# Attention scores of a first mixer: three products over 64 rows per head, two heads in turn on the array's row halves, in place of two products of stacked parts

## The chip, the core and the metric

The kernel runs on one core of a Trainium2 chip. Five engines work side by side, each through its own instruction queue in order: TensorE (PE, matrix products; its weight loads are shown apart as PEld), VectorE (DVE), ScalarE (ACT), GpSimd (POOL) and SyncE (SP, which here only starts transfers). The metric is the device time of one execution in microseconds (us). The kernel before takes 1453.77 us, the median of three runs that lie between 1453.04 and 1455.49 us. The profile was taken from one further execution.

## The reference, cut to what matters

The program is a two-layer streaming encoder on 512 tokens of width 1024, batch 1. Layer 0 starts with a mixer of two kinds of attention. Both have a query and key width of 64:

```
def forgetting_attention(q, k, v, log_f):          # 8 heads
    ...
        logits = jnp.einsum('bhqd,bhkd->bhqk', q_b, k, preferred_element_type=jnp.float32) * scale
        logits = logits + F_b[..., :, None] - F[..., None, :]
        logits = jnp.where(k_pos[None, :] <= q_pos[:, None], logits, NEG_INF)
        p = jax.nn.softmax(logits, axis=-1)
        return jnp.einsum('bhqk,bhkd->bhqd', p.astype(v.dtype), v)

def differential_attention(q1, q2, k1, k2, v, lam): # 4 heads, two score maps each
    ...
        l1 = jnp.einsum('bhqd,bhkd->bhqk', q1_b, k1, preferred_element_type=jnp.float32) * scale
        l2 = jnp.einsum('bhqd,bhkd->bhqk', q2_b, k2, preferred_element_type=jnp.float32) * scale
        p1 = jax.nn.softmax(jnp.where(mask, l1, NEG_INF), axis=-1)
        p2 = jax.nn.softmax(jnp.where(mask, l2, NEG_INF), axis=-1)
        p = p1 - lam * p2
        return jnp.einsum('bhqk,bhkd->bhqd', p.astype(v.dtype), v)
```

The change touches only how `q·k` of these two is formed. The rest of layer 0 (output projection, cross-attention to a memory of 256 tokens, a gated feed-forward net) and layer 1 are as they were.

## The kernel before

**Precision.** A float32 operand `v` is split in two parts of the fast matrix format, `hi` (a rounded copy, made by ACT) and `lo = v - hi` (a subtraction on DVE, line 279). A product of two split operands is three products, hi·hi, hi·lo and lo·hi (`mm3`, lines 289 to 291). Nearly all matrix work of the program has this form.

**Scores.** A projection of q or k yields a 128 x 512 tile: 128 rows are the 64 channels of two heads (or of the two maps of a differential head) one above the other, and the 512 columns are tokens. There are 8 such pairs of tiles, 4 for the differential heads and 4 for the forgetting heads; the text calls each a q/k pair. `q_parts` (line 616) and `k_parts` (629) scale a projection's result into the tile `tmp` (lines 619 and 632) and then build operands for each head s that fill all 128 rows with parts: `qa` holds q-hi on the head's own 64 rows and q-lo on the other 64; `ka` holds k-hi twice; `kb` holds k-lo on the head's own rows and zeros on the others, which four MEMSETs at line 751 write once at the start. `p_soft` (657) then makes the scores of 128 queries against n = 128, 256, 384 or 512 keys (i = 0 to 3) with two full products: ka·qa gives hi·hi + hi·lo in one, kb·qa adds lo·hi (lines 669 and 670). A product has at least 256 columns. So one q/k pair takes, for each i, two heads times two products of 256, 256, 384 and 512 columns, and the stage has 8 x 4 = 32 such places.

**What follows a score.** One DVE instruction at line 676 adds the mask or bias, takes the row minimum and clears the bank of the result; ACT takes the exponential (682), DVE its reciprocal (683). Forgetting heads are normalised on DVE (909), differential pairs combined (841, 842), the result is turned by PE in 128 x 128 blocks (700, `ident`), copied (703, 705), and multiplied with v: full products at line 712 for the differential heads, and for the forgetting heads at line 922 products with 64 columns of weights, two heads in turn on the array's two column halves.

**Order.** All of this stage is put in order by a planner (`Plan`). Each piece of work has a priority, a guessed PE duration and guessed ACT and DVE times, and takes resources: two banks `s` for scores (shared with small helper products at 417, 452, 612), two banks `w`, eight score tiles `e`. Work without hurry, the next projections (`acc<-xh`, lines 289 to 291) and the products of the memory (`acc<-mem`), stands between the scores. On top of the planner's order the framework that builds the program moves an instruction back when what it waits for comes late. In the trace the stage lies between 0 and about 235 us; its scores lie between 48 and 219 us.

Of the kernel before, what the change touches and what calls it, by code (L numbers as in the profile page):

```python
# [237 lines left out]
class Builder:  # L238
# [377 lines left out]
    def q_parts(self, ps):  # L616
        nc, mp = self.nc, self.mp
        tq = self.til(mp, "tmp")
        nc.vector.scalar_tensor_tensor(out=folded(tq[:]), in0=restored(ps[:]), scalar=-0.125, in1=folded(self.rb[:]), op0=ALU.mult, op1=ALU.mult)
        out = []  # L620
        for s in range(2):
            a, b = slice(64 * s, 64 * s + 64), slice(64 - 64 * s, 128 - 64 * s)
            qa = self.til(mp, f"qa{s}", dtype=F32R, bufs=2)
            nc.scalar.copy(qa[a, :], tq[a, :])
            self.sub(qa[b, :], tq[a, :], qa[a, :])
            out.append(qa)
        return out

    def k_parts(self, ps, par):
        nc, mp = self.nc, self.mp  # L630
        tk = self.til(mp, "tmp")
        nc.vector.tensor_tensor(out=folded(tk[:]), in0=restored(ps[:]), in1=folded(self.rb[:]), op=ALU.mult)
        out = []
        for s in range(2):
            a, b = slice(64 * s, 64 * s + 64), slice(64 - 64 * s, 128 - 64 * s)
            ka = self.til(mp, f"ka{s}", dtype=F32R, bufs=2)
            kb = self.kbt[s][par]
            nc.scalar.copy(ka[a, :], tk[a, :])
            nc.scalar.copy(ka[b, :], tk[a, :])
            self.sub(kb[a, :], tk[a, :], ka[a, :])  # L640
            out.append((ka, kb))
        return out

    def p_qk(self, pl, dq, dk, par, kdeps, edeps, prio):
# [3 lines left out]
            pl, dq, self.xs, lambda ps: st.update(q=self.q_parts(ps)), (("D", 0.66), ("A", 0.52), ("D", 0.6), ("D", 0.6)), load=(("A", 0.52),),  # L648
# [3 lines left out]
            pl, dk, self.xs, lambda ps: st.update(k=self.k_parts(ps, par)), (("D", 0.6), ("A", 0.52), ("D", 0.6), ("D", 0.6)), load=(("A", 1.56),),  # L652
# [4 lines left out]
    def p_soft(self, pl, st, s, i, bias, deps, prio):  # L657

        nc, mp = self.nc, self.mp
        n = P * (i + 1)  # L660
        nn = max(n, 256)
        res = {}

        def score():
            qa, (ka, kb) = st["q"][s], st["k"][s]
            ps = self.bank("s")
            b = bias()
            qs = qa[:, i * P : (i + 1) * P]
            nc.tensor.matmul(banked(ps[:, :nn]), qs, alternate(ka[:, :nn]), start=True, stop=False)
            nc.tensor.matmul(banked(ps[:, :nn]), qs, alternate(kb[:, :nn]), start=False, stop=True)  # L670
            e = res["e"] = self.x[self.turns % 8]
            self.turns += 1
            got = restored(ps[:, :nn])
            to, got, b = (e[:, :n], got[:, 0, :], b) if n < nn else (folded(e[:, :n]), got, folded(b))
            sm = res["sm"] = self.til(self.sp, "sm", (P, 4), bufs=12)
            nc.vector.tensor_tensor_reduce(
                out=to, in0=got, in1=b, scale=1.0, scalar=3.0e38, op0=ALU.add, op1=ALU.min, accum_out=sm[:, 0:1]
            )

        def expo():  # L680
# [4 lines left out]
        a = pl.add(score, 2 * MM * nn / 512, deps, prio, take=("s", "e"), free=("s",), chain=(("D", 0.07 + 0.54 * n / 512),))  # L685
        b = pl.add(expo, 0, [a], prio, chain=(("A", 0.3 + 0.4 * n / 512), ("D", 0.08)))
# [57 lines left out]
    def mix0(self):  # L744
        nc, t, tc = self.nc, self.t, self.tc
        with tc.tile_pool(name="mix0", bufs=1, reuse_waits="tile") as mp:
            self.mp = mp
            self.kbt = [[mp.tile([P, 512], F32R, name=f"kb{s}{i}") for i in range(2)] for s in range(2)]
            for s in range(2):
                for i in range(2):  # L750
                    nc.vector.memset(self.kbt[s][i][64 - 64 * s : 128 - 64 * s, :].bitcast(F32), 0.0)
# [72 lines left out]
            for h in range(4):  # L824
# [3 lines left out]
                st, qk = self.p_qk(pl, t["dq"][h], t["dk"][h], h % 2, xk, [norm], p)  # L828
# [3 lines left out]
                for i in range(4):  # L832
                    n = P * (i + 1)
                    bias = lambda n=n: dmask[:, 512 - n : 512]
                    r1, a1, b1 = self.p_soft(pl, st, 0, i, bias, qk, p + SOFT_PRIO)
                    r2, a2, b2 = self.p_soft(pl, st, 1, i, bias, qk, p + SOFT_PRIO)
# [8 lines left out]
                    ss += [a1, a2]  # L845
# [26 lines left out]
            for p_ in range(4):  # L872
# [4 lines left out]
                st, qk = self.p_qk(pl, t["fq"][p_], t["fk"][p_], p_ % 2, xk, [norm], p)  # L877
# [16 lines left out]
                for i in range(4):  # L894
                    n = P * (i + 1)
                    for h, s, pt, fb, b, got, ts in items:

                        def bias(i=i, n=n, fb=fb):
                            fm = self.til(mp, "tb")
                            nc.gpsimd.affine_select(  # L900
                                out=fm[:, :n], in_=fb["b"][:, :n], pattern=[[-1, n]], compare_op=ALU.is_ge, fill=BIG, base=i * P, channel_multiplier=1
                            )
                            return fm[:, :n]

                        r1, a1, b1 = self.p_soft(pl, st, s, i, bias, qk + [b], p + SOFT_PRIO)

                        def norm1(r1=r1, n=n):
                            e, sm = r1["e"], r1["sm"]
# [925 lines left out]
```

## Time and profile before

| what | value |
|---|---|
| median of three runs | 1453.77 us (1453.04 to 1455.49) |
| the profiled execution | 1455.27 us |
| its span, from the first to the last instruction | 1453.5 us |
| PE busy | 1427.1 us, 98% |
| DVE busy | 1193.3 us, 82% |
| ACT busy | 801.7 us, 55% |
| mean granted PE clock | 0.998 |

The profiled execution is 1.5 us slower than the median, and 1.8 us of its time lie outside the span. A change in the trace is therefore added to 1455.27 us for the profiled execution and to 1453.77 us for the median.

How to read the rows: `L669` is line 669 of the kernel; `s<-ka,qa` is a product of the moving tile ka and the weights qa into a bank s; `128*128 128x256` are the rows and columns of the weights and the size of the moving tile. Matrix products overlap in the array, so a product's duration (0.38 us for 512 columns) is longer than the time that it takes from the engine. That is read from one start to the next, and the text calls it a slot.

### The profile page before, as it was taken

The numbers are of one execution on the slowest core, as the hardware profiler recorded it, in microseconds if no ns is written. First come the engines' busy times: TensorE is split into PE (matmuls) and PEld (weight loads), VectorE is DVE, ScalarE is ACT, GpSimd is POOL, SyncE is SP. The second block draws the span as 40 slices with busy tenths as digits, with TensorE's granted clock in tenths as the row PEclk, the third lists the DMA queues.
The fourth block names the chain that finished last, engine by engine and source line by source line (L and its number), as shares of the span: only waits on it lengthen the run. The fifth ranks groups of instructions, "written<-read, shape, count | busy, mean of one in ns | idle before, by whom it ended". The sixth has DMA issues, their size and how long they took to land.

```text
span 1453.5 us, 22202 instructions
## 1 busy us (share of the span) xinstructions
PE 1427.1 (98%) x8330; PEld 1267.4 (87%) x8330; DVE 1193.3 (82%) x2255; ACT 801.7 (55%) x1345; POOL 57.9 (4%) x100
## 2 busy tenths in 40 slices
PE   9999999999999999999999999999999999999998
PEld 7888868899889999899888788889988899999987
DVE  7778886766689999999778868676667999999975
ACT  7767574444466555545456734444445655555544
POOL 0000120000001000000000100000000000000000
PEclk9999999999999999999999999999999999999999
DMA  5222304324248666542332232323323756564322
GB/s 200 88 73 73 102 32 158 117 86 131 87 138 196 172 156 166 145 131 66 94 103 87 74 102 78 111 91 127 117 87 123 200 156 168 159 160 133 89 70 80
DMA packets 60796, 171.74 MB, mean 118 GB/s; under 512 B 6673, under 2 KB 6673, under 8 KB 60689
## 3 DMA queue, kind: packets, MB, share of 16 engines
q1 hardware_dynamic: 55072, 152.43, 32.3%
q0 software_dynamic: 4608, 16.78, 6.9%
q8 instruction: 65, 1.06, 0.3%
q10 hardware_dynamic: 1008, 1.12, 0.2%
q14 instruction: 43, 0.34, 0.1%
HBM read 168.21 MB, written 2.10 MB: 117 GB/s over the span
## 4 chain that ended last, share of the span: by engine, by line
PE 68%; DVE 22%; issue 4%; ACT 4%; DMA 1%; POOL 0%; DVEq 0%; ACTq 0%; POOLq 0%
PE acc L289 13%; PE acc L291 13%; PE acc L290 13%; DVE wl L279 5%; DVE c L1281 4%; PE w L289 3%; PE w L290 3%; PE w L291 3%; PE acc L351 2%; PE s L289 2%; PE acc L352 2%; PE acc L353 2%; PE s L291 2%; PE s L290 2%; PE w L1621 1%
## 5 line engine op out<-in xcount | busy, mean ns | idle before, releaser
L289 PE MATMUL acc<-xh,wh 128*128 128x512 f32 (+1 forms) x832 | 293.3, 353 | 0.1
L291 PE MATMUL acc<-xh,wl 128*128 128x512 f32 (+1 forms) x832 | 289.1, 347 | 1.3 <-DVE wl L279 1.3
L290 PE MATMUL acc<-xl,wh 128*128 128x512 f32 (+1 forms) x832 | 289.0, 347 | 0.0
L279 DVE TENSOR_TENSOR wl<-raw,wh 128x1024 fp32r<-128x1024 f32 (+2 forms) x201 | 240.6, 1197 | 39.3 <-ACT wh L282 35.8
L282 ACT CAST wh<-raw 128x1024 fp32r<-128x1024 f32 (+2 forms) x137 | 140.3, 1026 | 156.2 <-PE acc L290 96.7
L291 PEld LDWEIGHTS acc<-xh,wl 128*128 128x128 f32 x832 | 158.2, 190 | 16.8 <-DVE wl L279 1.6
L289 PEld LDWEIGHTS acc<-xh,wh 128*128 128x128 f32 x832 | 158.2, 190 | 15.4 <-ACT v L1393 0.3
L290 PEld LDWEIGHTS acc<-xl,wh 128*128 128x128 f32 x832 | 158.2, 190 | 15.0
L1281 DVE SCALAR_TENSOR_TENSOR c<-hs,vec,c 128x512 f32<-128x512 f32 x176 | 129.3, 750 | 5.1 <-ACT c L1274 4.6
L289 PE MATMUL w<-ah,wh 128*128 128x512 f32 x304 | 115.6, 380 | 0.0
L291 PE MATMUL w<-ah,wl 128*128 128x512 f32 x304 | 115.3, 379 | 0.0
L290 PE MATMUL w<-al,wh 128*128 128x512 f32 x304 | 115.3, 379 | 0.0
L1274 ACT ACTIVATE c<-hs,vec 128x512 f32<-128x512 f32 x88 | 69.7, 812 | 56.5 <-DVE hs L1419 49.2
L291 PEld LDWEIGHTS w<-ah,wl 128*128 128x128 f32 x304 | 57.5, 189 | 8.1
L289 PEld LDWEIGHTS w<-ah,wh 128*128 128x128 f32 x304 | 57.7, 190 | 7.2 <-ACT c L1289 0.5
L290 PEld LDWEIGHTS w<-al,wh 128*128 128x128 f32 x304 | 57.7, 190 | 6.7
L289 PE MATMUL acc<-mem,wh 128*128 128x256 f32 (+1 forms) x192 | 60.3, 314 | 0.0
L291 PE MATMUL acc<-mem,wl 128*128 128x256 f32 (+1 forms) x192 | 59.8, 311 | 0.0
L290 PE MATMUL acc<-mem,wh 128*128 128x256 f32 (+1 forms) x192 | 59.6, 311 | 0.0
L512 DVE TENSOR_TENSOR x<-w,x 128x512 f32<-128x512 f32 x72 | 49.5, 688 | 9.1 <-PE w L291 9.1
L1183 ACT CAST wh<-dr 128x512 fp32r<-128x512 f32 x64 | 39.4, 615 | 31.1 <-PE w L290 15.3
L512 DVE TENSOR_TENSOR x<-acc,x 128x512 f32<-128x512 f32 x32 | 22.1, 691 | 40.4 <-PE acc L291 40.4
(373 smaller groups left out, 3758.5 us busy)
## 6 DMA issues: line engine op xcount, KB each, us to landing
raw<-in_up_dram SPq DMA_DIRECT2D x56, 512.0 KB, 3.3
dr<-in_down_dram SPq DMA_DIRECT2D x64, 256.0 KB, 2.9
sa<-in_up_dram SPq DMA_DIRECT2D x32, 512.0 KB, 4.2
sa<-in_up_dram POOLq DMA_DIRECT2D x32, 512.0 KB, 5.5
raw<-in_xk_dram SPq DMA_DIRECT2D x16, 512.0 KB, 3.3
raw<-in_wo_dram SPq DMA_DIRECT2D x16, 512.0 KB, 3.2
raw<-in_xq_dram SPq DMA_DIRECT2D x16, 512.0 KB, 3.3
raw<-in_xv_dram SPq DMA_DIRECT2D x16, 512.0 KB, 3.2
```

Of the source, the lines that this page charges most:

```text
L279: self.nc.vector.tensor_tensor(out=lo, in0=v, in1=hi.bitcast(F32), op=ALU.subtract)
L282: self.nc.scalar.copy(hi, v)
L289: mm(out, wh, xh, start=first, stop=False, skip_group_check=parts)
L290: mm(out, wh, xl, start=False, stop=False, skip_group_check=parts)
L291: mm(out, wl, xh, start=False, stop=last, skip_group_check=parts)
L351: mm(ps, xh[k][:, ts], wh, start=(k == 0), stop=False)
L352: mm(ps, xh[k][:, ts], wl, start=False, stop=False)
L353: mm(ps, xl[k][:, ts], wh, start=False, stop=(k == 7))
L512: self.nc.vector.tensor_tensor(out=x, in0=restored(ps[:]), in1=x, op=ALU.add)
L1183: nc.scalar.copy(st["wh"][:, :cols], st[tag][:, :cols])
L1274: nc.scalar.activation(st["c_"][:, j, :], hs()[:, j, 2:514], AF.Identity, scale=self.col("cw", (layer * 3 + 2) * 44 + blk), bias=self.col( ...
L1281: nc.vector.scalar_tensor_tensor(out=c, in0=hs()[:, j, n : n + 512], scalar=w, in1=c, op0=ALU.mult, op1=ALU.add)
```

## The change

The parts stay in the plain form: `qh`, `ql`, `kh`, `kl`, 128 x 512 each, one ACT copy and one DVE subtraction for q, and the same for k. A score is three products with the 64 rows of its own head: rows 0 to 63 for one, 64 to 127 for the other. The two heads of a q/k pair are now one piece of work in the planner: it takes both `s` banks and two `e` tiles at once, emits the six products in turn between the heads, each placed on the row half of the array (`tile_position=(64 * s, 0)`), and then the two DVE reductions. The planner counts 3 slots of PE for it where it counted 2 + 2.

```
-        out = []
-        for s in range(2):
-            a, b = slice(64 * s, 64 * s + 64), slice(64 - 64 * s, 128 - 64 * s)
-            qa = self.til(mp, f"qa{s}", dtype=F32R, bufs=2)
-            nc.scalar.copy(qa[a, :], tq[a, :])
-            self.sub(qa[b, :], tq[a, :], qa[a, :])
-            out.append(qa)
-        return out
-
-    def k_parts(self, ps, par):
...
-            nc.scalar.copy(ka[a, :], tk[a, :])
-            nc.scalar.copy(ka[b, :], tk[a, :])
-            self.sub(kb[a, :], tk[a, :], ka[a, :])
-            out.append((ka, kb))
-        return out
+        return self.qk_parts("q", tq)
+
+    def k_parts(self, ps):
+        tk = self.til(self.mp, "tmp")
+        self.nc.vector.tensor_tensor(out=folded(tk[:]), in0=restored(ps[:]), in1=folded(self.rb[:]), op=ALU.mult)
+        return self.qk_parts("k", tk)
+
+    def qk_parts(self, tag, v):
+        hi, lo = (self.til(self.mp, tag + i, dtype=F32R) for i in "hl")
+        self.split(hi[:], lo[:], v[:])
+        return hi, lo
...
-            nc.tensor.matmul(banked(ps[:, :nn]), qs, alternate(ka[:, :nn]), start=True, stop=False)
-            nc.tensor.matmul(banked(ps[:, :nn]), qs, alternate(kb[:, :nn]), start=False, stop=True)
...
+            ps = [self.bank("s") for _ in range(2)]
+            bs = [bias() for bias in biases]
+            for c, (q, k) in enumerate(((0, 0), (1, 0), (0, 1))):
+                for s in range(2):
+                    rows = slice(64 * s, 64 * s + 64)
+                    nc.tensor.matmul(
+                        banked(ps[s][:, :nn]), st["q"][q][rows, i * P : (i + 1) * P], alternate(st["k"][k][rows, :nn]), start=(c == 0), stop=(c == 2),
+                        tile_position=(64 * s, 0),
+                    )
+            for s in range(2):
...
-        a = pl.add(score, 2 * MM * nn / 512, deps, prio, take=("s", "e"), free=("s",), chain=(("D", 0.07 + 0.54 * n / 512),))
-        b = pl.add(expo, 0, [a], prio, chain=(("A", 0.3 + 0.4 * n / 512), ("D", 0.08)))
+        a = pl.add(score, 3 * MM * nn / 512, deps, prio, take=("s", "s", "e", "e"), free=("s", "s"), chain=(("D", 0.07 + 0.54 * n / 512),) * 2)
+        b = [pl.add(lambda r=r: expo(r), 0, [a], prio, chain=(("A", 0.3 + 0.4 * n / 512), ("D", 0.08))) for r in res]
...
-            self.kbt = [[mp.tile([P, 512], F32R, name=f"kb{s}{i}") for i in range(2)] for s in range(2)]
-            for s in range(2):
-                for i in range(2):
-                    nc.vector.memset(self.kbt[s][i][64 - 64 * s : 128 - 64 * s, :].bitcast(F32), 0.0)
```

Three places of the programs show what the new order is. The first is PE's queue at the first score of the first differential head (i = 0). Before, between two groups of projection products:

```order
L291 MATMUL acc_83_501<-xh_28_218,wl_496 128x512
L669 MATMUL s_521<-ka_78_487,qa_71_448 128x256
L670 MATMUL s_521<-kb_110,qa_71_448 128x256
L669 MATMUL s_526<-ka_79_491,qa_72_451 128x256
L670 MATMUL s_526<-kb_112,qa_72_451 128x256
L289 MATMUL acc_83_501<-xh_30_224,wh_496 128x512
```

And after, where 501 and 502 are the two heads' banks:

```order
L291 MATMUL acc_83_487<-xh_23_197,wl_483 128x512
L658 MATMUL s_501<-kh_477,qh_440 128x256
L658 MATMUL s_502<-kh_477,qh_440 128x256
L658 MATMUL s_501<-kh_477,ql_441 128x256
L658 MATMUL s_502<-kh_477,ql_441 128x256
L658 MATMUL s_501<-kl_478,qh_440 128x256
L658 MATMUL s_502<-kl_478,qh_440 128x256
L289 MATMUL acc_83_487<-xh_25_203,wh_482 128x512
```

Four full products have become six on row halves, and full products stand on both sides of them. Of the 32 places 24 keep the strict turn of the heads, three begin with two products of one head, and five have all three products of one head ahead of the other's. The second place is one of these five, in PE's queue at the second q/k pair of the forgetting heads. Before, a head's two products stood by themselves, with turns (`ident`) between the heads:

```order
L289 MATMUL acc_495_2274<-mem_1590,wh_2351 128x256
L669 MATMUL s_1956<-ka_304_1536,qa_288_1469 128x256
L670 MATMUL s_1956<-kb_113,qa_288_1469 128x256
L700 MATMUL w_1965<-ident,x_139 128x128 x4
L669 MATMUL s_1974<-ka_303_1532,qa_287_1466 128x256
L670 MATMUL s_1974<-kb_111,qa_287_1466 128x256
```

After, banks 1937 and 1938 of one place (i = 0):

```order
L290 MATMUL acc_529_2447<-mem_1650,wh_2442 128x256
L692 MATMUL w_1957<-ident,x_131 128x128 x2
L658 MATMUL s_1937<-kh_1520,qh_1506 128x256
L658 MATMUL s_1937<-kh_1520,ql_1507 128x256
L658 MATMUL s_1937<-kl_1521,qh_1506 128x256
L692 MATMUL w_1957<-ident,x_131 128x128
L658 MATMUL s_1938<-kh_1520,qh_1506 128x256
L658 MATMUL s_1938<-kh_1520,ql_1507 128x256
L658 MATMUL s_1938<-kl_1521,qh_1506 128x256
```

The heads are apart here, and one place makes two excursions to the row halves. In all the 32 places stand in 38 unbroken runs. Counting each boundary in PE's queue between full products, column halves (line 922) and row halves, there were 14 before, all at line 922, and there are 79 after.

The third place is DVE's queue at the first q/k pair. Before, with two subtractions of 64 x 512 each for q and for k:

```order
L619 SCALAR_TENSOR_TENSOR tmp_446<-acc_69_421,rb_325 128x512
L279 TENSOR_TENSOR wl_561<-raw_559,wh_560 128x1024
L279 TENSOR_TENSOR qa_71_448<-tmp_446,qa_71_448 64x512
L279 TENSOR_TENSOR qa_72_451<-tmp_446,qa_72_451 64x512
L632 TENSOR_TENSOR tmp_485<-acc_76_460,rb_325 128x512
L279 TENSOR_TENSOR wl_625<-raw_623,wh_624 128x1024
L279 TENSOR_TENSOR kb_110<-tmp_485,ka_78_487 64x512
L279 TENSOR_TENSOR kb_112<-tmp_485,ka_79_491 64x512
```

After:

```order
L619 SCALAR_TENSOR_TENSOR tmp_438<-acc_69_413,rb_317 128x512
L279 TENSOR_TENSOR wl_552<-raw_550,wh_551 128x1024
L279 TENSOR_TENSOR ql_441<-tmp_438,qh_440 128x512
L624 TENSOR_TENSOR tmp_475<-acc_76_450,rb_317 128x512
L279 TENSOR_TENSOR wl_631<-raw_629,wh_630 128x1024
L279 TENSOR_TENSOR kl_478<-tmp_475,kh_477 128x512
```

One subtraction of 128 x 512 stands where two of 64 x 512 stood. ACT's queue loses four copies per q/k pair: two of q become one, four of k become one. The queue of GpSimd keeps its order; in SyncE's queue the two loads of the memory and the loads of the first output weights shift by a few places against the loads of the projections.

73 lines of the change are left out of this document (31 added, 42 removed).

## The prediction

> **What bounds the kernel now.** I read the page's busy times first, then the stage of the scores in stretches of 10 us, then single products of PE in the timeline. The page:
>
> ```profile
> PE 1427.1 (98%) x8330; PEld 1267.4 (87%) x8330; DVE 1193.3 (82%) x2255; ACT 801.7 (55%) x1345; POOL 57.9 (4%) x100
> PE 68%; DVE 22%; issue 4%; ACT 4%; DMA 1%; POOL 0%; DVEq 0%; ACTq 0%; POOLq 0%
> ```
>
> PE bounds the program: 98% busy, and 68% of the chain that ended last. So each slot that PE gains or loses counts in full, except where PE waits anyway. In the stage of the scores it waits little. These are all its waits over 0.1 us there, from the view of waits between 80 and 230 us, and two of the 10 us stretches with the lowest granted clock (columns: stretch, length, busy time and number of instructions of PE, PEld, DVE, ACT, POOL, then PE's clock, DMA share, GB/s):
>
> ```profile
> PE w L700 <- DVE x L909: 1.6, 2, 1.4
> PE s L452 <- DVE sqt L446: 1.3, 4, 0.4
> PE s L669 <- DVE sm L676: 1.0, 2, 0.7
> PE w L700 <- DVE sm L683: 0.2, 1, 0.2
> ...
> 190.00:200.00 10.00, 8.16 (x51) 5.73 (x49) 9.22 (x31) 9.73 (x25) 2.79 (x6) 0.94 0.01 2
> 200.00:210.00 10.00, 10.00 (x61) 7.48 (x61) 7.76 (x25) 4.90 (x15) 1.72 (x4) 0.89 0.16 53
> ```
>
> The waits sum to 4.1 us in 150 us, all of them for DVE. A clock of 0.94 and 0.89 costs 0.06 x 10 + 0.11 x 10 = 1.7 us more. So at most 5.8 us of the stage are to be had from DVE and ACT; the rest is PE's own work.
>
> **The products themselves (term A).** Slots, from start to start in the timeline:
>
> ```profile
> 48.04 0.28 PE L670 MATMUL s<-kb,qa 128*128 128x256 f32 x1
> 48.15 0.28 PE L669 MATMUL s<-ka,qa 128*128 128x256 f32 x1
> ...
> 51.58 0.33 PE L670 MATMUL s<-kb,qa 128*128 128x384 f32 x1
> 51.74 0.33 PE L669 MATMUL s<-ka,qa 128*128 128x384 f32 x1
> ...
> 57.36 0.38 PE L669 MATMUL s<-ka,qa 128*128 128x512 f32 x1
> 57.57 0.38 PE L670 MATMUL s<-kb,qa 128*128 128x512 f32 x1
> ```
>
> A slot is 0.11, 0.16 and 0.21 us for 256, 384 and 512 columns. Per q/k pair the four places have widths of 256, 256, 384 and 512 columns, 0.59 us for one product of each; four products make 2.36 us, and 8 pairs 18.9 us. The change makes six of the four. If two halves run at the same time, six cost three slots: 14.2 us, a gain of 4.7. If they run one after the other, six slots: 28.3 us, a loss of 9.4. No product on row halves stands in this trace. The nearest rows are the products on column halves, line 922:
>
> ```profile
> 182.87 0.28 PE L670 MATMUL s<-kb,qa 128*128 128x256 f32 x1
> 183.08 1.07 PE L922 MATMUL w<-pt,v 128*64 128x512 f32 x2
> 184.08 0.43 PE L669 MATMUL s<-ka,qa 128*128 128x384 f32 x1
> 184.34 0.33 PE L670 MATMUL s<-kb,qa 128*128 128x384 f32 x1
> 184.60 2.37 PE L922 MATMUL w<-pt,v 128*64 128x512 f32 x14
> 186.90 0.33 PE L700 MATMUL w<-ident,x 128*128 128x128 f32 x1
> ...
> 94.78 0.38 PE L353 MATMUL acc<-wh,xl 128*128 128x512 f32 x1
> 94.99 2.32 PE L712 MATMUL w<-pt,v 128*128 128x512 f32 x8
> 97.15 0.27 PE L700 MATMUL w<-ident,x 128*128 128x128 f32 x1
> ```
>
> Plain float32 products are two records each. At line 712 four of them on the whole array, 512 + 384 + 256 + 128 = 1280 columns, take 97.15 - 94.99 = 2.16 us. At line 922 the x14 are one of 512 columns and two each of 384, 256 and 128, 2048 columns; one after the other they would take 2.16 x 2048 / 1280 = 3.46 us, but they take 186.90 - 184.60 = 2.30, which is the 2.16 of the busier half and a little. Column halves do run together, and I take the same for row halves. The Trainium skill, "TensorE: Matmul & The Clock Gate", Part 3, says that products on different row groups run at the same time, their starts about 4 ns apart; by that rule alone the sum would be the gain of 4.7 us, and no run here shows it for rows.
>
> The gain is not whole: in five of the 32 places (two of 512 columns, three of 256) the program has all three products of one head first. They need three slots more each: 2 x 3 x 0.21 + 3 x 3 x 0.11 = 2.3 us. Term A: -4.7 + 2.3 = **-2.4 us**.
>
> **The switches (term B).** The same rows show what it costs to change between the whole array and halves. The product at 182.87 has a slot of 0.11 and would let the next start at 182.98; line 922 starts at 183.08, 0.10 later. One product of 512 columns would take 2.16 x 512 / 1280 = 0.86 us; back on the whole array, 184.08 is 1.00 later, 0.14 more: 0.05 for its weights, which could not be loaded ahead, and about 0.10 for the change back. The product at 184.08 then holds PE for 0.26 us instead of 0.16: again 0.10 for weights, now of 128 columns. At 184.34 + 0.16 = 184.50 the next change begins, and line 922 starts at 184.60. So a change costs 0.10, and 0.10 more for 128 columns of weights that come in the open; the row halves have 128 columns as well. I price a switch at 0.20 us. From below it is bounded by the whole-array change to line 712 at 94.99, 0.21 after the product ahead and so without any gap: 0. The Trainium skill, "TensorEngine Tiling (Array Packing)", Key Properties, has a rule against this change: switching the tiling mode drains the engine. The trace agrees with its 0.10 us of gap; the page gives no price.
>
> The order has 79 boundaries where 14 stood: 65 x 0.20 = 13.0 us. Against it stands what the scores pay now: the first product of a score often shows its weight load in the open, because it waited for its bank:
>
> ```profile
> L669 PE MATMUL s<-ka,qa 128*128 128x256 f32 (+2 forms) x64 | 22.4, 356 | 1.1 <-DVE sm L676 1.0
> L670 PE MATMUL s<-kb,qa 128*128 128x256 f32 (+2 forms) x64 | 20.0, 317 | 0.0
> ```
>
> The first is 356 - 317 = 39 ns longer than the second, x 64 = 2.5 us, which the switches replace. Term B: 13.0 - 2.5 = **+10.5 us**.
>
> **DVE and ACT (term C).** Between 0 and 230 us:
>
> ```profile
> L279 DVE TENSOR_TENSOR qa<-tmp,qa 64x512 fp32r<-64x512 f32 x16 | 11.0, 687 | 0.7 <-ACT qa L624 0.2
> L279 DVE TENSOR_TENSOR kb<-tmp,ka 64x512 fp32r<-64x512 f32 x16 | 10.9, 684 | 0.5 <-ACT ka L638 0.2
> L279 DVE TENSOR_TENSOR qa<-w,qa 128x512 fp32r<-128x512 f32 x1 | 0.7, 693 | 2.7 <-ACT qa L282 2.7
> L639 ACT CAST ka<-tmp 64x512 fp32r<-64x512 f32 x16 | 9.9, 617 | 0.4
> L638 ACT CAST ka<-tmp 64x512 fp32r<-64x512 f32 x16 | 9.9, 616 | 0.8 <-DVE tmp L632 0.6
> L624 ACT CAST qa<-tmp 64x512 fp32r<-64x512 f32 x16 | 9.8, 614 | 2.8 <-PE s L670 1.5 <-DVE tmp L619 1.1
> ...
> 195.13 0.38 PE L290 MATMUL acc<-ml,wh 128*128 128x512 f32 x1
> 196.93 0.63 PE L700 MATMUL w<-ident,x 128*128 128x128 f32 x4 [1.42 <-DVE x L909]
> 197.89 0.38 PE L669 MATMUL s<-ka,qa 128*128 128x256 f32 x1 [0.33 <-DVE sm L676]
> ...
> 194.54 0.69 DVE L279 TENSOR_TENSOR qa<-tmp,qa 64x512 fp32r<-64x512 f32 x1
> 195.70 0.68 DVE L279 TENSOR_TENSOR kb<-tmp,ka 64x512 fp32r<-64x512 f32 x1
> 196.31 0.47 DVE L909 TENSOR_SCALAR x<-x,sm 128x512 f32<-128x512 f32 x1
> 196.81 0.69 DVE L279 TENSOR_TENSOR kb<-tmp,ka 64x512 fp32r<-64x512 f32 x1
> ```
>
> A subtraction of 128 rows costs 693 ns, one of 64 rows 684 to 687, so 16 of the 32 subtractions go with their time, 11.0 us of DVE, and 32 of the 48 copies, 32 x 0.62 = 19.8 us of ACT. Nearly all of that lies beside PE's work, since PE waits 4.1 us only. What comes out of it is seen at the longest wait. The normalisation at 196.31, for which PE waits 1.42 us, has the second half of q's subtraction ahead of it (194.54), which the change removes: -0.69. The reduction for which PE waits the next 0.33 us stands behind the second half of k's (196.81), also removed: -0.33. The other waits I leave as they are. The low clock begins with these waits, and I take it that its 1.7 us go with them. Term C: -0.7 - 0.3 - 1.7 = **-2.7 us**, between 0 and -5.8.
>
> **Two banks at once (term D).** A score now takes both banks, so the next score of the pair cannot start for one head while DVE still reduces the other. The nearest row is PE's present wait for a reduction at line 669, 1.0 us in all. Above, one reduction of some 0.45 us at 12 places of the forgetting heads makes 5.4; below, 0, since the program let single heads go ahead where a bank comes late (the five places of term A). I take 0 and keep 5.4 for the range. The four MEMSETs at line 751 count nothing: they are over at 3.4 us, and the first scaling of x waits for a transfer until 3.8:
>
> ```profile
> 1.19 2.20 DVE L751 MEMSET kb<- 64x512 f32 x4 [0.18 <-issue]
> ...
> 0.73 3.08 DMA vec<-in_vec_dram
> ```
>
> GpSimd's queue is unchanged, and the shifted loads of memory and output weights are 0.5 MB each with tens of us ahead of their use: 0.
>
> **The sum.** -2.4 + 10.5 - 2.7 + 0 = +5.4 us. The profiled execution, 1455.27, would become 1460.7; against the median, 1.5 lower, 1453.77 + 5.4 = 1459.2, **1459 us**.
>
> **The rivals.**
> 1. Row halves run one after the other. Term A is +9.4 instead of -2.4: 11.8 more, 1471.0 us. For it: no row shows row halves. Against it: line 922.
> 2. Switches are cheap, and the kernel gets faster. If weights for the halves are loaded ahead, or the drain is shorter for rows, the switch costs less than 0.20. At 0.10, term B is 6.5 - 2.5 = +4.0, the sum -1.1: 1452.7. At 0 it is -2.5, the sum -7.6: 1446.2. The sum is zero at (2.4 + 2.5 + 2.7) / 65 = 0.12 us, and below 0.07 us the kernel is faster by over 0.2%. For it: no row prices a change to row halves, and at 94.99 another kind of product follows without any gap. Against it: the gap of 0.10 shows at each change to and from line 922 that is quoted.
> 3. Weights bound the halves. Now a product of 256 columns just hides its weight load in a slot of 0.11. If the loads of the two halves go one after the other, a pair of products takes 0.22 whatever its width: 3 x (0.22 - 0.11) x 16 + 3 x (0.22 - 0.16) x 8 = 6.7 us more, 1465.9.
> 4. Both banks late: term D at 5.4, 1464.6. For it: the pair now moves in step. Against it: 1.0 us of such waits today.
>
> **How the numbers follow.** The forecast (halves together, switches at 0.15 to 0.25, 1455 to 1464 us) gets 0.45; serial halves 0.14; cheap switches 0.22, half of it near 1446 and half near 1453; weights 0.11; late banks 0.08. What a measurement of this kernel can tell from no change is about 0.2%, 2.9 us. Faster than 1450.9: the cheaper half of rival 2 and small parts of the other half and of the forecast, 0.19. Slower than 1456.7: 0.64. The rest, 0.17, is same. The range leaves out the free switches below and the upper end of serial halves above: 1448 to 1472.
>
> **What will show it.** At the new score line: if term A is right, two records start together and 6 of 512 columns take 0.65 us and not 1.3; if B is right, about 0.10 us of gap ahead of each run and behind it, and a first product 0.10 longer on each side; if C is right, 16 subtractions of q and k less, no wait of over 0.7 us near the end of the scores, and a clock of 1.00 there. The prediction is wrong if the switch is not near 0.20, if halves do not overlap, or if the forgetting heads run into new waits for both banks.

## The result and the profile after

The kernel after takes 1456.63 us, the median of 22 runs (1455.78 to 1457.96), against 1453.88 us for the kernel before (22 runs, 1452.48 to 1457.84). The ratio is 1.0018, with a 95% interval of 1.0012 to 1.0024: 2.75 us slower. The sign was forecast, the size is half of the 5.4 us. At 0.19% it lies a hair inside the 0.2% that the prediction called the least that can be told; with 22 runs of each it is told from no change.

The busy times on the page of the kernel after:

```profile
PE 1431.5 (98%) x8394; PEld 1264.5 (87%) x8394; DVE 1179.9 (81%) x2235; ACT 783.3 (54%) x1313; POOL 57.6 (4%) x100
```

PE has 4.4 us more to do, DVE 13.4 and ACT 18.4 us less. All waits of PE over 0.1 us in the stage of the scores (80 to 230 us):

```profile
PE s L452 <- DVE sqt L446: 0.6, 1, 0.6
```

Before they summed to 4.1 us. The stretches that had a clock of 0.94 and 0.89:

```profile
190.00:200.00 10.00, 9.89 (x71) 7.48 (x67) 9.49 (x32) 6.97 (x16) 2.31 (x4) 1.00 0.17 54
200.00:210.00 10.00, 9.86 (x70) 7.27 (x70) 9.17 (x39) 6.13 (x20) 2.96 (x6) 1.00 0.16 55
```

The clock is 1.00 in both. Of the DVE and ACT work that q and k need, this is left (groups by line, 0 to 230 us):

```profile
L279 DVE TENSOR_TENSOR kl<-tmp,kh 128x512 fp32r<-128x512 f32 x8 | 5.5, 684 | 0.0
L279 DVE TENSOR_TENSOR ql<-tmp,qh 128x512 fp32r<-128x512 f32 x8 | 5.5, 683 | 0.0
L282 ACT CAST kh<-tmp 128x512 fp32r<-128x512 f32 x8 | 4.9, 617 | 2.0 <-PE s L658 1.2 <-DVE tmp L624 0.8
L282 ACT CAST qh<-tmp 128x512 fp32r<-128x512 f32 x8 | 4.9, 617 | 1.1 <-PE s L658 1.1
```

11.0 us of subtractions instead of 21.9, and 9.8 us of copies instead of 29.6, as the prediction counted. PE's timeline after, with two runs of six products on row halves (line 658), one of 256 and one of 512 columns, and then products with v (now line 911) and one place where the heads are apart:

```profile
49.16 0.38 PE L291 MATMUL acc<-xh,wl 128*128 128x512 f32 x1
49.47 0.38 PE L658 MATMUL s<-kh,qh 64*128 64x256 f32 x2
49.69 0.28 PE L658 MATMUL s<-kh,ql 64*128 64x256 f32 x2
49.80 0.28 PE L658 MATMUL s<-kl,qh 64*128 64x256 f32 x2
50.00 0.48 PE L289 MATMUL acc<-xh,wh 128*128 128x512 f32 x1
50.32 0.38 PE L290 MATMUL acc<-xl,wh 128*128 128x512 f32 x1
...
78.63 0.38 PE L291 MATMUL acc<-xh,wl 128*128 128x512 f32 x1
78.94 0.49 PE L658 MATMUL s<-kh,qh 64*128 64x512 f32 x2
79.26 0.38 PE L658 MATMUL s<-kh,ql 64*128 64x512 f32 x2
79.47 0.38 PE L658 MATMUL s<-kl,qh 64*128 64x512 f32 x2
79.78 0.48 PE L289 MATMUL acc<-xh,wh 128*128 128x512 f32 x1
80.10 0.38 PE L290 MATMUL acc<-xl,wh 128*128 128x512 f32 x1
...
181.71 0.48 PE L658 MATMUL s<-kh,qh 64*128 64x512 f32 x1
...
182.55 0.38 PE L291 MATMUL acc<-mem,wl 128*128 128x256 f32 x1
...
189.23 2.37 PE L911 MATMUL w<-pt,v 128*64 128x512 f32 x16
191.54 0.43 PE L658 MATMUL s<-kh,qh 64*128 64x384 f32 x1
```

Read the pairs first. "x2" with a duration of 0.28 is two products of 256 columns in the time of one: both halves run at the same time. From 79.26 to 79.47 two of 512 columns take one slot of 0.21. Now the edges. The full product at 49.16 has a slot of 0.22 us and would let the next start at 49.38; the run starts at 49.47, so 0.09 of gap. The first pair's slot is 49.69 - 49.47 = 0.22 instead of 0.11: 0.11 of open weight load. The last pair starts at 49.80 and would be done at 49.91; the full product starts at 50.00, 0.09 later, and holds PE for 0.32 instead of 0.22, again 0.10 for its weights. That is some 0.40 us for a run, 0.20 for a switch. So the run of 256 columns takes 50.32 - 0.22 - 49.38 = 0.72 us of PE with its edges, where four full products took 4 x 0.11 = 0.44. The run of 512 columns takes 80.10 - 0.22 - (78.63 + 0.22) = 1.03, where four took 0.86. At 181.71 one head's three products alone take as long as the six at 78.94 (182.55 - 181.71 = 0.84).

The whole program is longer than the stage that changed, so I took as a marker the first common PE product behind the stage, the first `s<-kth,qh` of the next part. In PE's timeline before:

```profile
286.03 0.27 PE L289 MATMUL s<-kth,qh 128*128 128x256 f32 x1
```

And after:

```profile
286.65 0.27 PE L289 MATMUL s<-kth,qh 128*128 128x256 f32 x1
```

At this marker the kernel after is 0.62 us late, not 2.75. But the two profiles do not stand at the same clock. That of the kernel before has one stretch of low clock ahead of the marker, seen here in a view cut to it (the clock is the third number from the end):

```profile
198.71:202.13 3.42, 3.42 (x7) 0.97 (x9) 1.61 (x10) 1.29 (x6) 0.88 (x2) 0.50 0.00 0
```

At a clock of 0.50 for 3.42 us PE loses 1.7 us. The profile of the kernel after has no such stretch, so at equal clock the marker is 0.62 + 1.7 = 2.3 us late, and most of the 2.75 us arises ahead of it. How often the low clock comes can be told from the mean granted clock that is listed for each execution. The four profiles with such a stretch (before, before again, e2 and e7) list 0.998, the other nine 0.999 or 1.000. Of 70 more executions of the kernel before, run beside the experiments, 25 list 0.998 or less and take 1455.5 us in the mean, 45 list 0.999 or more and take 1453.5. Of the 22 of the kernel after only one lists 0.998; the others take 1456.6 us. If the 22 executions of the kernel before in the result are like these 70 (their clocks are not listed), the medians compare executions that mostly have no low clock. Without it the kernel after is 3.1 us slower. The experiments carry two numbers: the median of the runs, and the marker.

### The profile page after: what moved, and what is told of

It reads as the page before. It is cut to its first block, busy times and chain, and to the rows that moved or that the text cites. A ratio compares the mean times of both kernels' runs of the same rounds, so it can differ in the third digit from the quotient of the medians.

```text
span 1455.1 us, 22270 instructions
## 1 busy us (share of the span) xinstructions
PE 1431.5 (98%) x8394; PEld 1264.5 (87%) x8394; DVE 1179.9 (81%) x2235; ACT 783.3 (54%) x1313; POOL 57.6 (4%) x100
## 4 chain that ended last, share of the span: by engine, by line
PE 70%; DVE 20%; issue 4%; ACT 3%; DMA 2%; POOL 0%; SPq 0%; DVEq 0%; ACTq 0%; POOLq 0%
PE acc L289 14%; PE acc L291 13%; PE acc L290 13%; DVE wl L279 5%; DVE c L1270 4%; PE w L289 3%; PE w L290 3%; PE w L291 3%; PE acc L351 2%; PE acc L352 2%; PE acc L353 2%; PE s L289 2%; PE s L290 2%; PE s L291 2%; PE s L658 2%
## 5 line engine op out<-in xcount | busy, mean ns | idle before, releaser
L1172 ACT CAST wh<-dr 128x512 fp32r<-128x512 f32 x64 | 39.4, 615 | 29.6 <-PE w L290 15.3
```

What stands on the lines that cost most here:

```text
L1172: nc.scalar.copy(st["wh"][:, :cols], st[tag][:, :cols])
```

## The experiments

Of each run: the start of the marker in its profile, what the profiled execution took behind it, and the median with the ratio to the kernel before on the same chip. The markers of before, before again, e2 and e7 hold one stretch of low clock, 1.7 us; the others hold none.

| kernel | marker, us | profiled execution less marker, us | median, us | ratio (95%) |
|---|---|---|---|---|
| before | 286.0 | 1169.3 | 1453.88 | 1 |
| before, again | 286.2 | 1167.4 | 1453.61, one run | |
| after | 286.7 | 1170.2 | 1456.63 | 1.0018 (1.0012 to 1.0024) |
| after, again | 286.5 | 1171.6 | 1458.13, one run | |
| e1 | 282.2 | 1169.7 | 1452.51 | 0.9991 (0.9982 to 1.0000) |
| e2 | 291.1 | 1170.9 | 1462.55 | 1.0061 (1.0047 to 1.0074) |
| e3 | 284.5 | 1170.6 | 1455.14 | 1.0006 (0.9997 to 1.0015) |
| e4 | 296.3 | 1170.9 | 1466.74 | 1.0084 (1.0069 to 1.0099) |
| e5 | 285.7 | 1170.8 | 1455.18 | 1.0008 (0.9999 to 1.0018) |
| e7 | 290.3 | 1168.9 | 1457.48 | 1.0021 (1.0011 to 1.0030) |
| e8 | 280.9 | 1170.3 | 1449.76 | 0.9970 (0.9957 to 0.9982) |
| e9 | 284.4 | 1168.7 | 1452.33 | 0.9984 (0.9975 to 0.9993) |
| e10 | 282.2 | 1170.0 | 1451.99 | 0.9982 (0.9973 to 0.9991) |

The marker repeats to 0.2 us. What lies behind it moves by 1 to 2 us from kernel to kernel, without a change in its work.

**Do the halves run together? (e4)** The kernel after, with both heads' products on the upper half; what is computed for the second head is left out.

```diff
-                    rows = slice(64 * s, 64 * s + 64)
+                    rows = slice(0, 64)
...
-                        tile_position=(64 * s, 0),
+                        tile_position=(0, 0),
```

> The kernel after with both heads' products on the same row half (rows 0 to 63 of the tiles for both, so the second head's scores are those of the first head: its part of the computation is left out). Number, size and order of the products and all switches stay. Theory (the two halves run together): the six products of a place now take six slots and not three, where the heads took turns; 28.3 us for all scores against 14.2 + 2.3 with the halves, 11.8 us slower than after, 1468.4 us, ratio to before 1.010. Rival (the halves do not really run together, the records only start together): as after, 1456.6, ratio 1.002.

Measured: 1466.74 us, 10.1 more than after, and 9.6 at the marker. The second run in PE's timeline:

```profile
49.41 0.38 PE L291 MATMUL acc<-xh,wl 128*128 128x512 f32 x1
49.72 0.48 PE L658 MATMUL s<-kh,qh 64*128 64x256 f32 x2
...
50.59 0.48 PE L289 MATMUL acc<-xh,wh 128*128 128x512 f32 x1
```

From 49.72 to 50.59 is 0.87 us, where the halves take 50.00 - 49.47 = 0.53: three slots of 0.11 more. The serial halves of rival 1 look like this, and the kernel after does not.

**What does a switch cost? (e5)** The same six products on the whole array, without any switch; they mix the two heads.

```diff
-                    rows = slice(64 * s, 64 * s + 64)
+                    rows = slice(0, 128)
...
-                        tile_position=(64 * s, 0),
```

> The kernel after with each of the six products on the whole array (all 128 rows of qh, ql, kh, kl for both heads, so a score is the sum of two heads' scores: the parting of the heads is left out). No product on row halves is left, so 65 of the 79 switches go; the six products take six slots as with both heads on one half. Theory (a switch costs 0.20 us): 65 x 0.20 = 13.0 us less than with both heads on the same half, some 2.5 us given back for weight loads that stand in the open after waits: 1455.4 to 1458 us, ratio to before 1.001 to 1.003. Rival (the switches cost half or are hidden): 6.5 us less or fewer, 1462 us or more, ratio over 1.0055.

Measured: 1455.18 us. The second run there:

```profile
49.58 0.38 PE L291 MATMUL acc<-xh,wl 128*128 128x512 f32 x1
49.79 0.39 PE L658 MATMUL s<-kh,qh 128*128 128x256 f32 x2
50.01 0.39 PE L658 MATMUL s<-kh,ql 128*128 128x256 f32 x2
50.24 0.39 PE L658 MATMUL s<-kl,qh 128*128 128x256 f32 x2
50.46 0.38 PE L289 MATMUL acc<-xh,wh 128*128 128x512 f32 x1
```

No gap and no open load at either end: six full products take 50.46 - 49.79 = 0.67 us, less than the 0.72 of the six on halves. Both e4 and e5 do six products one after another. Counted in the order of starts in the two traces, e4 has 79 boundaries and e5 has 8, so 71 switches lie between them, not the 65 of the expectation, which counts the 14 of the kernel before as left. They cost 1466.74 - 1455.18 = 11.6 us, 0.16 per switch; by the marker 10.6 and 0.15. Rival 2 (0.10 or less) is out. The row halves save some 10 us (e4 against after) and their switches cost some 11 (e4 against e5). The change would have been 1.0 (marker) to 1.4 us (medians) better with six plain products, if zeros could stand on the other head's rows for nothing.

**Fewer switches (e3).** The kernel after with the scores of i = 0 and i = 1 made as one run, both in the two halves of the same two banks: 68 boundaries instead of 79.

```diff
-    def p_soft(self, pl, st, i, biases, deps, prio):
+    def p_soft(self, pl, st, iis, biases, deps, prio):
...
+            for at, i in enumerate(iis):
+                nn = max(size(i), 256)
+                for c, (q, k) in enumerate(((0, 0), (1, 0), (0, 1))):
+                    for s in range(2):
+                        rows = slice(64 * s, 64 * s + 64)
+                        out[i, s] = ps[s][:, 256 * at : 256 * at + nn]
```

> The kernel after with the scores of i = 0 and i = 1 (256 columns each) in one piece of work, in the two halves of the same two banks. The program has 68 boundaries between full array, column halves and row halves in place of 79. Theory (a switch costs 0.20 us and is on PE's path): 11 x 0.20 = 2.2 us faster than after, 1454.4 us, ratio to before 1.0004. Rival (switches are hidden in waits): no gain, 1456.6, or slower where four reductions now hold the banks longer, up to 1459.

Measured: 1455.14 us, 1.5 less than after, and 2.2 less at the marker. For 11 switches that is 0.14 to 0.20 each, near the price from e4 and e5. The run also joins four reductions to one piece of work, which is not parted from the switches here.

**The relief of DVE and ACT given back (e2).** The kernel after, with 2 subtractions and 4 copies of 64 x 512 more per q/k pair, whose results nothing reads.

```diff
         self.split(hi[:], lo[:], v[:])
+        more = [self.til(self.mp, f"more{i}", dtype=F32R, bufs=1) for i in range(2)]
+        for _ in range(1 if tag == "q" else 3):
+            self.nc.scalar.copy(more[0][0:64, :], v[0:64, :])
+        self.sub(more[1][0:64, :], v[0:64, :], hi[0:64, :])
```

> The kernel after, plus the DVE and ACT work that the change took away: per q/k pair two more subtractions of 64 x 512 on DVE and four more copies of 64 x 512 on ACT, into tiles that nobody reads. Products and their order in the plan stay. Theory (PE's waits fell from 4.1 to 0.6 us, and the clock stayed at 1.00, because DVE and ACT had less to do): the waits come back, 3 to 5 us slower than after, 1459.6 to 1461.6 us, ratio to before 1.004 to 1.0055. Rival (the waits went because the scores stand in another order): within 1 us of after, ratio 1.002.

Measured: 1462.55 us, 5.9 more than after and 4.4 at the marker. PE's waits between 80 and 230 us:

```profile
PE s L662 <- DVE sm L672: 2.6, 1, 2.6
PE s L452 <- DVE sqt L446: 0.6, 1, 0.6
```

The long wait is not one of those of the kernel before: it ends at 87.66 us, and a stretch of low clock follows it.

```profile
89.41:92.82 3.41, 3.41 (x11) 2.68 (x10) 3.39 (x12) 2.87 (x10) 0.00 (x0) 0.50 0.00 0
```

So 2.0 of the 4.4 us at the marker are waits and 1.7 are clock; four of the five executions of e2 list a clock of 0.998 or less, which makes its median that much longer. Work of DVE and ACT that lies almost wholly beside PE is worth 2.7 us here at equal clock, where the prediction gave it 1.0, and it brings the low clock back. With it given back, the change costs 8.5 us by the medians and 5.1 at the marker, where both profiles have one stretch of low clock.

**The relief alone (e8).** The kernel before, with the parts of the first head used for the second head too; the second head's scores are left out.

```diff
-        for s in range(2):
+        for s in range(1):
             a, b = slice(64 * s, 64 * s + 64), slice(64 - 64 * s, 128 - 64 * s)
...
-        return out
+        return out * 2
```

> The kernel before with the stacked parts of the first head alone, used for both heads (the second head's scores are those of the first; its parts are left out): per q/k pair one DVE subtraction and one ACT copy less for q, one subtraction and two copies less for k. All products stay on the whole array in the order of before. Theory (DVE's and ACT's load is what PE waits for at the end of the scores): PE's waits of 4.1 us fall to 1 to 2 us and the low clock at 190 to 210 us goes, 3 to 5 us faster than before, 1449 to 1451 us, ratio 0.9965 to 0.998. Rival (only the new order of the row-half kernel avoided the waits): within 1 us of before, ratio 0.9995 to 1.0005.

Measured: 1449.76 us, 3.9 less than before, and 5.1 at the marker. PE's waits between 80 and 230 us:

```profile
PE s L452 <- DVE sqt L446: 1.3, 4, 0.4
PE s L669 <- DVE sm L676: 0.2, 1, 0.2
```

And the two stretches that had the low clock:

```profile
190.00:200.00 10.00, 9.85 (x68) 7.51 (x67) 9.43 (x34) 7.80 (x20) 2.94 (x6) 1.00 0.01 3
200.00:210.00 10.00, 9.90 (x68) 7.49 (x67) 8.66 (x34) 7.39 (x21) 4.53 (x8) 1.00 0.22 66
```

The waits fall from 4.1 to 1.5 us, and the 1.7 us of low clock are gone: 4.3 of the 5.1 us. At equal clock the relief is 3.4 us at the marker. e8 relieves ACT a little less than the change does: three copies per q/k pair are left out, against four.

**The products with v (e1).** In the trace before, three of the four pairs of forgetting heads have one product with v alone (183.08, 1.00 us), then scores, then the other seven (184.60, 2.30 us); after, all eight stand together in 2.31 us (189.23). That is not the same in all four pairs: the fourth of the kernel before has its eight in one piece but takes 2.94 us, and the second of the kernel after takes 2.66.

```profile
224.63 3.00 PE L922 MATMUL w<-pt,v 128*64 128x512 f32 x16
227.57 0.48 PE L289 MATMUL acc<-mh,wh 128*128 128x512 f32 x1
...
202.12 2.73 PE L911 MATMUL w<-pt,v 128*64 128x512 f32 x16
204.78 0.43 PE L658 MATMUL s<-kh,qh 64*128 64x384 f32 x2
```

The edit makes the kernel before keep them together, with one small full product (of no use) into the bank ahead of them.

```diff
                     ps = self.bank("w")
+                    nc.tensor.matmul(ps[:, 510:512], pts[0]["t"][:, 1024:1152], pts[1]["t"][:, 1150:1152], start=True, stop=True)
```

> The kernel before with one edit: ahead of the products of the forgetting heads with v on the column halves (line 922) stands one small full product that reads both heads' turned scores, so that the eight products come in one piece; before, the first of them stood alone at three of the four q/k pairs with a score between. Its result is overwritten. Theory (part of the after kernel's time comes from these products being together, not from the scores): in the trace before, the lone product takes 1.00 us and the other seven 2.30, together 3.30 against 2.3 in one piece, and the score between pays a switch and an open weight load, 0.3; 3 x 1.3 = 3.9 us gained, less 4 x 0.2 for the small products: 3.1 us faster than before, ratio 0.998. Rival (the shorter time of these products in the trace after is only the clock that was not lowered there): no gain, 0 to 0.8 us slower, ratio 1.000.

Measured: 1452.51 us, 1.6 less than the 1454.07 of the kernel before on the same chip, and 3.8 less at the marker. One block of PE's timeline in it:

```profile
184.17 0.28 PE L918 MATMUL w<-pt,pt 128*128 128x2 f32 x2
184.38 2.37 PE L923 MATMUL w<-pt,v 128*64 128x512 f32 x16
186.68 0.33 PE L700 MATMUL w<-ident,x 128*128 128x128 f32 x1
```

And the longest of PE's waits between 80 and 230 us:

```profile
PE s L669 <- DVE sm L676: 2.2, 3, 1.2
```

All eight in 2.30 us, and the other three pairs the same to 0.01 us. The clock is 1.00 at 190 to 210 us, so 1.7 of the 3.8 us at the marker are clock and 2.1 are left; PE's waits rise from 4.1 to 4.8 us, so part of the gain comes back as waits. Half of the expected 3.1 us came out by the medians, at the edge of the interval. So this order is worth 1 to 2 us by itself in the kernel before, and the kernel after has it without having asked for it. Why the planner's order came out so there is not settled: e2, with DVE as loaded as before, has it too.

**The low clock (e6).** The kernel before once more, for its profile.

> The kernel before once more, for a second profile. Theory (the low clock of 0.94 and 0.89 between 190 and 210 us hangs on where PE's wait of 1.4 us falls and is not in every run): the waits of PE between 80 and 230 us again 3.5 to 4.5 us; if the clock stays near 1.00 there, the span is 1.5 to 2 us shorter than in the first profile, about 1451.7 us. Rival (the clock falls every time): again 0.94 and 0.89, and a span of 1453.5.

The same two stretches in that profile:

```profile
190.00:200.00 10.00, 8.16 (x51) 5.79 (x50) 9.34 (x32) 9.73 (x24) 2.66 (x6) 0.95 0.01 2
200.00:210.00 10.00, 10.00 (x60) 7.52 (x60) 7.76 (x25) 4.90 (x15) 1.84 (x4) 0.87 0.15 53
```

0.95 and 0.87 where the first profile had 0.94 and 0.89, with the same waits ahead of them. So both profiles have it at the same place. It is still not in every execution, as the listed clocks say: 45 of 70 executions of this kernel list 0.999 or more. The expectation's theory was right in that, and the second profile alone does not show it.

**The rest of the time (e7, e11).** Behind the marker, where both kernels have the same work, the kernel after loses 0.9 us more in the first pair of profiles, and 4.2 in the second pair. A second profile of it (e11) was taken first to see whether that repeats.

> The kernel after once more, for a second profile. Theory (the stage's shift is fixed by the program, the late load of the memory by the place of the instruction load): the first product behind the stage starts within 0.3 us of the first profile, and ACT waits again about 1 us for the load at 793 to 795 us. Rival (both are chance): the start differs by over 1 us, or the load lands in 3.1 us.

It does: 286.5 at the marker, and 1171.6 behind it. The place that can be seen is near 793 us. ACT's timeline there in the kernel after:

```profile
794.55 0.42 ACT L482 ACTIVATE sq<-raw 128x256 f32<-128x256 f32 x1 [1.13 <-DMA raw<-in_mem_dram]
```

The DMA view of the 20 us around it (queues and their packets, then transfers with KB and us to landing):

```profile
q8 instruction: 1, 0.02, 0.6%
...
raw<-in_mem_dram SPq DMA_DIRECT2D x1, 512.0 KB, 5.1
```

and the same transfer in the kernel before, where ACT does not wait:

```profile
raw<-in_mem_dram SPq DMA_DIRECT2D x1, 512.0 KB, 3.1
```

A load of 512 KB lands after 5.1 us instead of 3.1, and ACT waits 1.13 us for it (1.33 in the second profile). Near 807 us PE waits for DVE, 1.0 and 1.1 us in the two profiles of after, and not in those of before. In the same 20 us one packet of instructions goes through the DMA engines, which does not in the kernel before. The packet records of the trace say more: this packet runs from 790.25 to 792.27 us; all but the last eight of the load's 4 KB packets are done by 792.45, and those eight follow one another until 794.05. If the packet's place in time depends on the length of the code ahead, then more instructions at the start should move it. e7 is the kernel after with 24 instead of 12 warming products at the start.

```diff
-WARM = 12
+WARM = 24
```

> The kernel after with 24 in place of 12 small products at the very start (line of WARM), where PE waits for the first transfer; the rest of the program comes 24 instructions later in PE's instruction stream. In the trace after, one packet of 16 KB on the queue of instructions takes 2.0 us at 790 us, on a DMA engine that also carries a load of the memory (the load takes 5.1 us and not 3.1), ACT waits 1.1 us for that load and PE 1.0 us a little later; the other variants of the row-half kernel show the same late step, no profile of the kernel before does. Theory (the place of instruction loads in the program costs this 1 us): the packet moves some 2.6 us earlier, the load lands in 3.1 us, PE's wait of 1.0 us near 806 us is gone, time 1.0 us less than after, about 1455.6, ratio 1.001. Rival (the late load has another cause): the wait stays, 1456.6 or, with a later start, up to 0.6 more.

Measured: 1457.48 us, not faster than after. The load is back at 3.2 us without a wait, and what lies behind the marker is 1168.9 us, 1.3 to 2.7 less than in the two profiles of after; PE's wait of 1.0 us is gone. But the marker itself is 3.6 us later: the scores begin 2.0 us later, and a low clock shows at another place, so that the total tells nothing. That stretch of e7:

```profile
180.00:190.00 10.00, 9.93 (x51) 7.79 (x49) 7.40 (x26) 5.98 (x11) 0.84 (x3) 0.83 0.32 106
```

The table above points the same way, though the two groups touch: the six profiles in which this step shows (after twice, e2 to e5) take 1170.2 to 1171.6 us behind the marker, 1170.8 in the mean; the other seven 1167.4 to 1170.3, mean 1169.2. That the packet holds the load back is argued from the two being there together and from the late packets; it was not undone by itself.

**Can one have the relief without the switches? (e9, e10)** e9 is the kernel before with the second head's subtractions on GpSimd, which is 4% busy; e10 has the edit of e1 as well.

```diff
-            self.sub(qa[b, :], tq[a, :], qa[a, :])
+            (nc.gpsimd if s else nc.vector).tensor_tensor(out=qa[b, :], in0=tq[a, :], in1=qa[a, :].bitcast(F32), op=ALU.subtract)
...
-            self.sub(kb[a, :], tk[a, :], ka[a, :])
+            (nc.gpsimd if s else nc.vector).tensor_tensor(out=kb[a, :], in0=tk[a, :], in1=ka[a, :].bitcast(F32), op=ALU.subtract)
```

> The kernel before with the second head's subtractions of q and k (16 of 32, 64 x 512 each) on GpSimd in place of DVE; products, copies and stacking stay. GpSimd is busy 4% of the time. Theory (DVE's load is what PE waits for at the end of the scores): a part of the 5 us that the stage gains when these subtractions and some copies are left out, 2 to 4 us faster than before, 1450 to 1452 us, ratio 0.997 to 0.9985. Rival (GpSimd is too slow for it, its subtraction holds up the weights of the products or the masks queued behind it): 0 to 5 us slower than before, ratio 1.000 to 1.0035.

> As the run before this one, with the small full product that keeps the eight products with v in one piece. Theory (both gains add): 1.5 us faster than with the subtractions moved alone, 1448.5 to 1450.5 us, ratio 0.996 to 0.9975. Rival (with DVE relieved the products stand together anyway and the small ones only cost): 0 to 1 us slower than with the subtractions moved alone.

Measured: 1452.33 and 1451.99 us, against 1454.89 for the kernel before on that chip: 0.9984 and 0.9982, both faster, with intervals that leave 1 out. The subtractions on GpSimd in e9:

```profile
L625 POOL TENSOR_TENSOR qa<-tmp,qa 64x512 fp32r<-64x512 f32 x8 | 12.6, 1578 | 101.3 <-ACT qa L624 48.6 <-DVE wl L279 40.2 <-DVE sm L676 7.9
L640 POOL TENSOR_TENSOR kb<-tmp,ka 64x512 fp32r<-64x512 f32 x8 | 12.2, 1530 | 29.1 <-ACT ka L638 12.6 <-DVE y L427 7.1 <-DVE sm L676 5.3
```

1.55 us each instead of 0.69, on an engine with time to spare. e10 beats both kernels; the two edits do not add up, since e10 gains only 0.3 us on e9, where 1.5 were expected. But much of this is the low clock, which ten of the 21 executions of before on that chip list: among the executions with 0.999 or more, e9 is 1.1 us faster (1452.2 against 1453.3) and e10 1.3. PE's waits did not fall in e9; they sum to 4.8 us. So moving DVE's subtractions alone does not show the relief that e8 and e2 show, which also take copies from ACT or give them back.

## Why the prediction was half right

- **Term A (products, -2.4).** The mechanism was right: pairs in one slot, six products of 512 columns in 0.84 us inside a run, of which 0.64 are the three slots. The gain of the halves over one after another was put at 11.8 and measured 9.6 to 10.1 us, so A was some 2 us too good.
- **Term B (switches, +10.5).** Right: 0.20 us per switch in the timeline, as read off line 922. Between e4 and e5 it is 0.15 to 0.16, less what e5 itself still pays for weight loads in the open; 65 of these make 9.7 to 10.6 us. The Trainium skill's rule that a change of tiling mode drains the engine ("TensorEngine Tiling (Array Packing)", Key Properties) agrees, with 0.09 us of gap at each edge; the open weight load costs as much again.
- **Term C (DVE and ACT, -2.7).** This step failed. "The other waits I leave as they are" was wrong: they fell from 4.1 to 0.6 us, not by 1.0. At equal clock e2 and e8 give 2.7 and 3.4 us for the relief. That a freed DVE brings each later reduction and normalisation in its queue forward, and not just the wait in front of which it stood, fits this but is not shown by itself: e9 freed DVE alone, and its waits stayed. The 1.7 us of clock went in the profile, as forecast. But they were subtracted from a median, and most executions of the kernel before do not have the low clock by their listed clocks, so they are not a full part of the measured difference.
- **Not in the sum: the products with v.** Three lone products of 1.00 us (at full clock) are gone, the fourth pair takes 2.30 us where it took 227.57 - 224.63 = 2.94, and the second pair takes 2.66 where its seven took 2.30 at full clock: 3 x 1.00 + 0.64 - 0.36 = 3.3 us. The order was read for the scores only; the switches at line 911 were counted, the time of the products between them was not.
- **Term D (both banks, 0).** Right: no wait for a score's bank is left in the list of waits, so rival 4 is out. Rival 3 (weight loads one after another) is out as well: the middle pair of 256 columns has a slot of 49.80 - 49.69 = 0.11.
- **The sum.** At the marker and at equal clock: +2.3 = A + B - 3.5 (waits) - 3.3 (products with v), so A + B is +9.1, where the prediction had 8.1. Behind the marker comes the late load, which the prediction did not have and of which PE's wait shows 1.0 us. Together 3.3 us, against 3.1 between the executions without low clock. The rest behind the marker is open; two profiles of one kernel differ there by as much (1169.3 and 1167.4).

So the forecast of +5.4 came out as +2.75 by errors of opposite sign, and that it came so near is in part luck: some 2.5 us of waits and 3.3 us of products with v better than thought, some 1 us in A and B, 1.7 us of clock and 1 us of the late load worse.

## What to carry to other kernels

A change between the whole array and its halves costs 0.15 to 0.2 us here, about half of it gap and half of it weights in the open, so a run on row halves has to be longer than the six products of 512 columns in this kernel before it beats the four stacked products. Work of DVE and ACT that seems hidden can be worth more than the waits in front of which it stands (2.7 to 3.4 us here, where the two longest waits gave 1.0); price it with all waits of the stage. Read the order of everything that shares the engine, not only of what was changed. Compare two versions at a common product right behind the changed stage: that marker repeated to 0.2 us where the whole time moved by 1 to 2. But compare the granted clock ahead of it first: here the profiles of before and after differed by 1.7 us of low clock, and by 0.62 us at the marker.

## What was not expected of the hardware

The low clock comes as one stretch of 3.4 us at 0.50: at 198.71 and 199.10 us in the two profiles of the kernel before, behind waits of PE of 1.42 and 0.33 us; at 89.41 us in e2, behind a wait of 2.64; and at 184.91 us in e7, which has no wait of PE over 0.6 us between 80 and 230 us. By the listed clocks it is in some executions of a kernel and not in others, 25 of 70 of the kernel before and 1 of 22 of the kernel after. What starts it is open. A subtraction of 64 x 512 costs GpSimd 1.55 us, where DVE takes 0.69. And a kernel's code can delay its own data: next to one packet of instructions a load of 512 KB took 5.1 us instead of 3.1.
